# A four-layer decoder trunk on one core: recurrent layer's weights one use ahead, state rows turned later, twelve small tiles for nine

## Chip, cores and metric

The kernel runs on one core of one Trainium2 chip. The metric is the device time of one execution in microseconds; several runs are taken and their median is given. Matmul operands are fp32 bits split into two halves (a rounded upper part and the remainder, both of type fp32r), so that each product of 128 rows takes three matmuls.

## What is computed

The reference is one inference step of four layers with the same skeleton, for 1024 prompt rows and 8 times 4 sample rows (1056 columns here, since the kernel holds activations transposed, features on partitions):

```python
for i in range(DEPTH):            # kinds: conv, attention, recurrent, conv
    mp, ... = mixer_of_kind(yp, ...)
    ms, ... = mixer_of_kind(ys, ...)
    yp = layer_norm(ALPHA * yp + mp, ln_g[i], ln_b[i])
    ys = layer_norm(ALPHA * ys + ms, ln_g[i], ln_b[i])

def rglru_mixer(...):             # the recurrent layer, "C"
    u, z = split(x @ w_in); uc = causal_dwconv(u, buf, conv_w) + conv_b
    r = sigmoid(uc blocks @ w_a + b_a); i = sigmoid(uc blocks @ w_x + b_x)
    a = exp(log_a(r)); b = sqrt(1 - a*a) * (i * uc)
    h = scan(a, b)                # h[t] = a[t]*h[t-1] + b[t]
    return (silu(z) * h) @ w_out, h[-1], last rows of u
```

The short-conv layer ("A") is `(silu(z) * b_gate * conv(c_gate * h)) @ w_out`. Each A and C layer also returns a few state rows (last rows before the convolution, last hidden state).

## The kernel before, in words

Features are cut into 8 chunks of 128 (index c), columns into 3 parts of 352 (index j). One **dense step** is 24 matmuls of 128x352: chunk c of the output for part j, over 8 input chunks, three matmuls each (`dense_steps`). The stages follow each other: layer A (`layer_a`), its out-projection with residual and norm (`out_phase`), layer B (attention), out-projection 1, layer C (`layer_c`, some 232 us), out-projection 2, the second layer A, and `final_phase`, the last out-projection, which turns its result to rows before the norm.

Order. All but the attention's core is recorded, not issued: every call goes through `Rec` (line 310 is where the recorded call is issued, so nearly all work has that line). Each recorded operation has a place in the record and a due time (its place, shifted by the constants in `AHEAD`). `Rec.lay` then walks a small model of the engines: an operation may start when its inputs are done and a buffer of its ring is free; of those able on an engine the one due first is taken. The order found is written out; each engine runs its list strictly in that order. SP issues nearly all transfers, in one list too.

Buffers are rings: `w` (3 tiles, split weights ready for TensorE), `ws` (5 tiles in the later layers, staging for weights, convolution inputs `g`, rows to be stored), `c` (small work tiles), `big` and `x` (18 tiles of a whole chunk); in PSUM `mm` (5 banks, dense steps) and `aux` (3 banks, convolution sums, transposes, statistics).

Weights. `load_w` loads 128 columns of weights into `ws`, ScalarE rounds them into `w` (CAST `w<-ws`), VectorE or GpSimd (by the table `WLO`) writes the remainder (TENSOR_TENSOR `w<-ws,w`). `layer_a` and `out_phase` record these loads two or three uses ahead; `layer_c` records each where it is used:

```python
W = self.get_w(("c", c), lambda: self.load_w(...))   # conv_in, line 1089
WA[n] = weights(n)                                   # gates, line 1135
W = self.load_w(win[:, D + c * P:...], ("z", c))     # gate_out, line 1185
```

`ORDER_C` (line 2211) lists the steps of layer C: `u` for `conv_in` of a chunk, `g` for its gates and scan, `z` for the gated output.

State rows. `put_rows` (line 935) turns the 18 or 36 columns of `SC` to rows by 8 transposes on TensorE into two `aux` banks, copies them to a `ws` tile on VectorE and stores them. `layer_a` and `layer_c` call it as their last step.

The final phase sums squares with `squares` (line 892): ScalarE squares three row pieces with an accumulator; the squared values go to a `c` tile of up to 512 columns and are not read.

Of the kernel before, what the change touches and what calls it, by code (L numbers as in the profile page):

```python
# [9 lines left out]
F32 = mybir.dt.float32  # L10
F32R = mybir.dt.float32r
I32 = mybir.dt.int32
AF = mybir.ActivationFunctionType
# [5 lines left out]
P = 128  # L19
D = 1024  # L20
# [478 lines left out]
class Trunk:  # L499
    def __init__(self, ctx, tc, io):  # L500
        self.ctx, self.tc, self.nc, self.io = ctx, tc, tc.nc, io
        self.rec = Rec(tc)

    @contextmanager
    def part(self):
# [25 lines left out]
        nc.vector.memset(self.ones_m, 1.0 / D)  # L531
        self.ones_r = ones

    def work(self, stack, nws, ncc):

        self.nwork = getattr(self, "nwork", 0) + 1
        self.nws = nws
        self.ws = Ring(self.rec, self.pool(f"ws{self.nwork}", nws, stack), "ws", nws) if nws else None
        self.wx = self.ws
        self.cc = Ring(self.rec, self.pool(f"c{self.nwork}", ncc, stack), "c", ncc)  # L540
# [16 lines left out]
    def wsl(self, w=1088, dt=F32):  # L557
        return self.ws.tile([P, 1088], dt, name="ws")[:, 0:w]

    def ct(self, w=512, dt=F32):  # L560
        return self.cc.tile([P, 512], dt, name="c")[:, 0:w]

    def cst(self, name, dst):
        a, b = COLS[name]
# [41 lines left out]
    def fetch(self, items):  # L606
        for key, fn in items:
            self.pre[key] = fn()
# [76 lines left out]
    def out_phase(self, pm, wsrc, U, X, ln, lp, res=None, done={}, spill=None, final=None, nxt=()):  # L685
# [3 lines left out]
        nc = self.nc  # L689
# [5 lines left out]
        W = {}  # L695
# [69 lines left out]

        running, late = [], {}
        for c, j in order:
            if c not in W:
                take(c)
            sl = slice(j * TC, (j + 1) * TC)  # L770
            xh, xl = X[c][:, 0, sl].bitcast(F32), X[c][:, 1, sl].bitcast(F32)
            k = kt[:, sl]
            if j == 0 and NCH - c <= self.nws - 2 and c >= 4:
                late[c] = self.wsl(T)
            y = done[c, j] if (c, j) in done else late[c][:, sl] if c in late else self.ct(TC)
            x = self.ct(TC)
            if (c, j) not in done:
                ps = self.mm(pm)[:, 0:TC]
                self.dense(ps, W[c], U, j, k if c else None)
                if res is None:  # L780
                    stt(out=ps, in0=xl, scalar=ALPHA, in1=ps, op0=ALU.mult, op1=ALU.add)
                    stt(out=y, in0=xh, scalar=ALPHA, in1=ps, op0=ALU.mult, op1=ALU.add)
                else:
                    nc.sync.dma_start(x, res[c][:, sl], rk=[("x", ln - 1, c, j)])
                    stt(out=y, in0=x, scalar=ALPHA, in1=ps, op0=ALU.mult, op1=ALU.add)
            if j == 2 and c >= 4:
                self.fetch(nxt[c - 4:c - 3])
            if c == 0:
                kp = self.aux(pm)[:, 0:TC]
                nc.tensor.matmul(kp, self.ones_m, y, start=True, stop=True)  # L790
                nc.scalar.activation(k, kp, AF.Copy, scale=-8.0 * NCH)
            d = ss[:, 0, sl] if c == 0 else y
            if c == 0 or (c, j) in done:
                stt(out=d, in0=k.bitcast(F32), scalar=0.125, in1=y, op0=ALU.mult, op1=ALU.add)
            if c == 0:
                nc.scalar.activation(ss[:, 1, sl], d, AF.Square)
            else:
                e0, e1 = (nc.gpsimd if c in s else nc.vector for s in SUMS[ln])
                e0.tensor_add(ss[:, 0, sl], ss[:, 0, sl], d)
                nc.scalar.activation(x, d, AF.Square)  # L800
                e1.tensor_add(ss[:, 1, sl], ss[:, 1, sl], x)
            if c not in late:
                nc.sync.dma_start(self.dd[c][:, sl], d, wk=[("d", ln, c, j)])
            for g in running:
                next(g, None)
            if c == NCH - 1:
                g = norm(j)
                next(g)
                running.append(g)
# [4 lines left out]
    def final_phase(self, pm, wsrc, U, X, ln, lp):  # L814


        nc, io = self.nc, self.io
# [6 lines left out]
        sq = lp.tile([P, 3, 3, 3], F32, name="fsq")  # L824
        W, R, gb = {}, {}, []

# [65 lines left out]
        def squares(j, n, c0, c1):  # L892
            nk = stat[:, j, 0:3]
            if n == 0:
                nc.vector.tensor_reduce(out=nk, in_=sm[:, j, 0:4].rearrange("p c i -> p i c"), axis=AX.X, op=ALU.add)
                nc.vector.tensor_scalar(out=nk, in0=nk, scalar1=-2.0 / D, scalar2=0.0, op0=ALU.mult, op1=ALU.add)
            for i in range(3):
                x = half(j, c0 // 4, i)[:, c0 % 4 * P:(c1 - 1) % 4 * P + P]
                nc.scalar.activation(self.ct((c1 - c0) * P), x, AF.Square, bias=nk[:, i:i + 1], accum_out=sq[:, j, i, n:n + 1])

        running = []
        for c, j in [(c, j) for c in range(4) for j in range(3)] + [(c, j) for j in range(3) for c in range(4, NCH)]:
            if c not in W:
                take(c)
            sl = slice(j * TC, (j + 1) * TC)
# [20 lines left out]
            if c == NCH - 1:  # L926
                g = norm(j)
# [19 lines left out]
    def layer_a(self, pm, a, X, lp, side=None, nxt=()):  # L947
        nc, io = self.nc, self.io
        stt = nc.vector.scalar_tensor_tensor
        win = io["a_w_in"][a]  # L950
# [69 lines left out]
            nc.vector.tensor_copy(SC[:, c, 2:18].rearrange("p (b t) -> p b t", t=2), gs[:, :, 4:6])  # L1020
        for _ in side or ():
            pass
        self.put_rows(pm, SC, 18, [(0, 2, io["o_conv_a_prompt"][a, 0]), (2, 18, io["o_conv_a_sample"][a].rearrange("b t f -> (b t) f"))])
        return U

    def first_a(self, a):
# [51 lines left out]
    def layer_c(self, pm, X, lp):  # L1078
# [7 lines left out]
        def conv_in(c, js):  # L1086

            if c not in UC:
                W = self.get_w(("c", c), lambda: self.load_w(win[:, c * P:(c + 1) * P], ("c", c)))
                g = self.wsl(1083)  # L1090
                nc.vector.memset(g[:, 0:3], 0.0)
                gs = g[:, 1027:1083].rearrange("p (b t) -> p b t", t=7)
                nc.vector.tensor_copy(gs[:, :, 0:3], self.PT[:, c, R_SC:R_SC + 24].rearrange("p (b t) -> p b t", t=3))
                uc = self.view2(self.big(F32R))
                UC[c], GT[c] = uc, (W, g, gs)
# [36 lines left out]
        def gates(c):  # L1132
            n, i = c // 2, c % 2
            if i == 0:
                WA[n] = weights(n)
                H[n] = self.big()[:, 0:2 * T].rearrange("p (a n) -> p a n", a=2)
            wax, h2, ucs = WA[n], H[n], (UC[c - i], UC[c - i + 1])
            rr, ii = [], []
# [43 lines left out]

        def gate_out(c):
            h2, i = H[c // 2], c % 2
            W = self.load_w(win[:, D + c * P:D + (c + 1) * P], ("z", c))
            u = self.view2(self.big(F32R))
            U[c] = u
            for j in range(3):
# [8 lines left out]

            nc.sync.dma_start(win_s[c, 0:508, :], cache[c, 4:512, :], rk=[("z", c)])
        UC, GT, WA, H = {}, {}, {}, {}
        win_s = io["o_nsa_win_sample"][0].rearrange("b t c g d -> b t (c g d)")  # L1200
        cache = io["cache_nsa_win"][0].rearrange("b t c g d -> b t (c g d)")
        for x in ORDER_C.split():
# [2 lines left out]
                conv_in(c, [int(j) for j in x[2:] or "012"])  # L1205
            else:
                (gates if x[0] == "g" else gate_out)(c)
        self.put_rows(pm, SC, 36, [(0, 3, io["o_lru_conv_prompt"][0, 0]), (3, 27, io["o_lru_conv_sample"][0].rearrange("b t f -> (b t) f")),
                                   (27, 28, io["o_lru_h_prompt"][0]), (28, 36, io["o_lru_h_sample"][0])])
        return U  # L1210

    def first_c(self):
# [1118 lines left out]
def trunk(ctx, tc, io, layers="ABCA"):  # L2331
# [37 lines left out]
            left = k.attend(B, bs, io["b_w_out"][0], xd)  # L2369
    with ExitStack() as c1:  # L2370
        lp = k.small(c1)
        k.work(c1, 5, 9)
        pm = banks(c1, "pm_1")
        k.rec.forget()
        k.later = 1
# [47 lines left out]
```

## Time and profile before

| | |
|---|---|
| median of 3 runs | 2428.99 us (2427.99 to 2431.45) |
| profiled execution | 2425.75 us, span of its records 2423.7 us |
| busy in the span | PE 2305.6, DVE 1583.6, ACT 1203.7, POOL 959.3 us |
| mean granted clock of TensorE | 0.977 of full speed |
| layer C, 1600 to 1832 us | PE 225.55, DVE 176.77, ACT 175.85, POOL 97.93 us |

The profile is one execution of the program. PE is TensorE's matmul, PEld its weight load, DVE VectorE, ACT ScalarE, POOL GpSimd, SPq the list of transfers on SyncE. A tile stands by its ring's name. Idle time before an instruction is put down to the work that ended it.

### The profile page before, as it was taken

To read this page: it belongs to the slowest core of one execution; us is meant where nothing else is said; L and a number is where in the kernel's file an instruction comes from. 1 tells how busy PE (TensorE), PEld (TensorE's weight loads), DVE (VectorE), ACT (ScalarE), POOL (GpSimd) and SP (SyncE) were. 2 spreads that over 40 slices of the span, in tenths; PEclk is the share of its full clock that TensorE was granted. 3 is DMA by queue.
4 is the path that set the end of the run, shared out by engine and by line. 5 is a ranking of instruction groups with operands and counts; after the bars stand their busy time and mean duration, and the time that the engine had idled before them with its cause. 6 is when DMAs were issued, how large, how long until landed. Compare 5 with 4: busy or idle time off the path is not lost. (4 is left out here: it accounts for less than half of the span.)

```text
span 2423.7 us, 41400 instructions
## 1 busy us (share of the span) xinstructions
PE 2305.6 (95%) x14801; PEld 2234.8 (92%) x14801; DVE 1583.6 (65%) x3686; ACT 1203.7 (50%) x2757; POOL 959.3 (40%) x1070
## 2 busy tenths in 40 slices
PE   8999997997989989999999999989999999999996
PEld 8999997996888879999999989989999999999996
DVE  5786875575358877777777777787765753433336
ACT  3211111234438878888888883487863442222233
POOL 3454543213137765565555552333463320000131
PEclk9999999997999999999999999999999999999998
DMA  7999988347356752111111234331113321111112
GB/s 260 351 350 338 321 291 281 98 151 245 104 175 230 247 201 56 33 47 43 47 48 41 78 123 124 117 103 53 53 47 118 99 67 53 44 44 53 35 46 72
DMA packets 334642, 320.34 MB, mean 132 GB/s; under 512 B 19462, under 2 KB 301542, under 8 KB 324964
## 3 DMA queue, kind: packets, MB, share of 16 engines
q1 hardware_dynamic: 325220, 250.58, 33.4%
q0 software_dynamic: 9216, 67.11, 7.4%
q8 instruction: 117, 1.92, 0.3%
q14 instruction: 89, 0.73, 0.1%
HBM read 237.31 MB, written 84.48 MB: 133 GB/s over the span
## 5 line engine op out<-in xcount | busy, mean ns | idle before, releaser
L310 PE MATMUL mm<-x,w 128*128 128x352 f32 x5760 | 948.9, 326 | 29.6 <-DVE ws L310 10.3
L310 PEld LDWEIGHTS mm<-x,w 128*128 128x128 f32 x5760 | 936.4, 190 | 36.6 <-DVE w L310 7.6
L310 PE MATMUL mm<-big,w 128*128 128x352 f32 x2208 | 375.4, 325 | 1.0 <-ACT c L310 1.0
L310 PEld LDWEIGHTS mm<-big,w 128*128 128x128 f32 x2208 | 357.2, 189 | 2.8 <-ACT c L310 1.3
L310 POOL TENSOR_TENSOR w<-ws,w 128x1024 fp32r<-128x1024 f32 (+1 forms) x43 | 104.8, 2438 | 445.8 <-ACT w L310 426.7
L1968 DVE TENSOR_TENSOR c<-T,c 128x512 fp32r<-128x512 f32 (+1 forms) x320 | 204.7, 648 | 49.3 <-ACT c L1964 44.9
L1964 ACT CAST c<-T 128x512 fp32r<-128x512 f32 (+1 forms) x320 | 174.3, 551 | 59.3 <-PE T L1960 37.7
L310 ACT CAST w<-ws 128x1024 fp32r<-128x1024 f32 (+2 forms) x116 | 120.3, 1038 | 163.3 <-PE mm L310 119.4
L641 PE MATMUL D<-x,w 128*128 128x352 f32 x1008 | 195.5, 330 | 2.2 <-DVE big L2095 2.2
L1870 PE MATMUL A<-big 128*128 128x320 f32 (+11 forms) x832 | 181.5, 334 | 3.4 <-DVE ast L1895 1.6
L1975 PE MATMUL O<-c,big 128*128 128x256 f32 x1056 | 180.4, 291 | 0.5 <-ACT c L1964 0.2
L310 POOL TENSOR_TENSOR big<-big,ws 128x1024 f32<-128x1024 f32 (+1 forms) x38 | 89.6, 2358 | 199.0 <-DMA big<-in_cache_nsa_kv,idx 103.9
L641 PEld LDWEIGHTS D<-x,w 128*128 128x128 f32 x1008 | 159.8, 188 | 5.7 <-DVE big L2095 3.5
L310 DVE TENSOR_TENSOR big<-big 128x256 f32<-128x256 f32 (+3 forms) x204 | 150.5, 758 | 21.7 <-POOL big L310 20.3
L310 DVE TENSOR_TENSOR w<-ws,w 128x1024 fp32r<-128x1024 f32 (+2 forms) x73 | 93.9, 1286 | 105.6 <-ACT w L310 104.8
L310 ACT CAST big<-aux 128x352 fp32r<-128x352 f32 (+3 forms) x116 | 45.4, 399 | 229.9 <-DVE aux L310 160.6
L1975 PEld LDWEIGHTS O<-c,big 128*128 128x128 f32 x1056 | 147.2, 189 | 2.5 <-DVE c L1968 0.7
L1928 POOL TENSOR_SCALAR pr<-pr,G,ast 128x32 f32<-128x32 f32 (+6 forms) x192 | 125.6, 668 | 47.1 <-DVE ast L1939 41.3
L1870 PEld LDWEIGHTS A<-big 128*128 128x128 f32 x832 | 134.3, 193 | 10.0 <-PE A L1870 2.2
L310 ACT ACTIVATE aux<-ws,PT 128x352 f32<-128x352 f32 (+2 forms) x72 | 42.7, 593 | 172.5 <-DVE ws L310 167.9
L1924 ACT ACTIVATE pr<-pr,ast 128x32 f32<-128x32 f32 (+6 forms) x192 | 118.4, 619 | 18.3 <-DVE ast L1895 17.4
L310 DVE SCALAR_TENSOR_TENSOR c<-c,mm 128x352 f32<-128x352 f32 x125 | 64.1, 515 | 92.3 <-ACT c L310 54.6
(286 smaller groups left out, 4032.7 us busy)
## 6 DMA issues: line engine op xcount, KB each, us to landing
ws<-in_a_w_in SPq DMA_DIRECT2D x64, 512.0 KB
raw<-big SPq DMA_DIRECT2D x128, 256.0 KB
big<-raw SPq DMA_DIRECT2D x128, 256.0 KB
c<-dd SPq DMA_DIRECT2D x48, 176.0 KB
xs<-x SPq DMA_DIRECT2D x24, 352.0 KB
x<-xs SPq DMA_DIRECT2D x8, 1056.0 KB
ws<-in_a_w_out SPq DMA_DIRECT2D x16, 512.0 KB
ws<-in_c_w_in SPq DMA_DIRECT2D x16, 512.0 KB
```

What stands on the lines that cost most here:

```text
L310: getattr(real, name)(*[f(x) for x in a], **{q: f(x) for q, x in k.items()})
L641: self.nc.tensor.matmul(ps, a, b, start=n == 0, stop=n == 23 and last)
L1870: nc.tensor.matmul(o, q[:, hl, i * P:(i + 1) * P], k, start=m == 0, stop=m == 1)
L1924: nc.scalar.activation(S[:, a:a + m], S[:, a:a + m], AF.Exp, bias=st[:, k:k + 1], scale=-1.0, accum_out=st[:, 3 + k:4 + k])
L1928: nc.gpsimd.tensor_scalar(S[:, a:a + m], S[:, a:a + m], G[:, i, 16 * k + h:16 * k + h + 1], st[:, 6 + k:7 + k], op0=ALU.mult, op1=ALU.mult)
L1964: nc.scalar.copy(x["H"][:, 0:n], x["tp"][:, 0:n])
L1968: nc.vector.tensor_sub(x["L"][:, 0:n], x["tp"][:, 0:n], x["H"][:, 0:n].bitcast(F32))
L1975: nc.tensor.matmul(O, v, M[:, y * P:(y + 2) * P], start=done[0] == 0, stop=done[0] == total - 1)
```

## The change

Four parts. (1) In layer C a table `todo` of all weight sets in order of use is made, and `take` records the set asked for and also the next one. (2) `put_rows` is no longer called at the end of a layer but kept as `self.rows` and called in the out-projection that follows, ahead of the step (c, j) = (2, 0). (3) In the layers after the attention a `c` tile has 384 columns instead of 512, and there are 12 instead of 9. (4) The unread squares of the final phase, up to 512 columns wide, go to an `aux` bank.

```diff
@@ out_phase, in the loop over (c, j)
+            if (c, j) == (2, 0) and self.rows:
+                self.rows()
+                self.rows = None
@@ final_phase
-                nc.scalar.activation(self.ct((c1 - c0) * P), x, AF.Square, bias=nk[:, i:i + 1], accum_out=sq[:, j, i, n:n + 1])
+                nc.scalar.activation(self.aux(pm)[:, 0:(c1 - c0) * P], x, AF.Square, bias=nk[:, i:i + 1], accum_out=sq[:, j, i, n:n + 1])
...
+            if (c, j) == (2, 0):
+                self.rows()
@@ layer_a (and layer_c likewise)
-        self.put_rows(pm, SC, 18, [(0, 2, io["o_conv_a_prompt"][a, 0]), (2, 18, io["o_conv_a_sample"][a].rearrange("b t f -> (b t) f"))])
+        self.rows = lambda: self.put_rows(pm, SC, 18, [(0, 2, io["o_conv_a_prompt"][a, 0]),
+                                                       (2, 18, io["o_conv_a_sample"][a].rearrange("b t f -> (b t) f"))])
@@ layer_c
-                W = self.get_w(("c", c), lambda: self.load_w(win[:, c * P:(c + 1) * P], ("c", c)))
+                W = take(("c", c))
...
-                WA[n] = weights(n)
+                WA[n] = take(("g", n))
...
-            W = self.load_w(win[:, D + c * P:D + (c + 1) * P], ("z", c))
+            W = take(("z", c))
...
+        def fetch(key):
+            w, c = key
+            if key not in self.pre:
+                self.pre[key] = weights(c) if w == "g" else self.load_w(win[:, (w == "z") * D + c * P:(w == "z") * D + (c + 1) * P], key)
+
+        def take(key):
+
+            fetch(key)
+            i = todo.index(key)
+            for k in todo[i + 1:i + 2]:
+                fetch(k)
+            return self.pre.pop(key)
@@ trunk
-        k.work(c1, 5, 9)
+        k.work(c1, 5, 12, 384)
```

The new record gives another order. At the end of the first layer A, TensorE's list before (-) and now (+), with `SC` the state columns, `mm<-big` the out-projection's dense steps and `aux<-c,ones_m` its column sums:

```order
 L310 MATMUL aux<-c 128x8
 L310 MATMUL mm<-x,w 128x352 x2226
-L310 MATMUL aux<-idf,SC 18x128 x8
 L310 MATMUL mm<-big,w 128x352 x36
 L310 MATMUL aux<-c,ones_m 128x352
```

The transposes have left the place between the layer's last dense step and the out-projection's first; they stand after its sixth step now. VectorE's list at the same place, where `big<-aux,big` writes the remainder of layer A's last output chunk, and `c<-x,mm` ends the first residual:

```order
 L310 TENSOR_TENSOR big<-aux,big 128x352
 L310 SCALAR_TENSOR_TENSOR c<-mm,c 128x352
-L310 COPY ws<-aux 18x512
 L310 TENSOR_TENSOR aux<-c,aux 128x320
-L310 COPY ws<-aux 18x512
+L310 TENSOR_TENSOR w<-ws,w 128x1024
 L310 TENSOR_TENSOR big<-aux,big 128x320
 L310 TENSOR_TENSOR aux<-c,aux 128x8x4
+L310 SCALAR_TENSOR_TENSOR mm<-x,mm 128x352
 L310 TENSOR_TENSOR big<-aux,big 128x32
-L310 SCALAR_TENSOR_TENSOR mm<-x,mm 128x352
 L310 SCALAR_TENSOR_TENSOR c<-x,mm 128x352
```

Both copies are gone from here, and a weight remainder has come in ahead of the last pieces. TensorE's list where layer C begins, before, with buffer numbers (`w_17980` and `w_17853` are the sets of chunks 1 and 0; `mm_18125` is their part j = 1, `mm_18272` and `mm_18284` are j = 2):

```order
L310 MATMUL mm_18125<-x_17915,w_17853 128x352 x3
L310 MATMUL mm_18125<-x_17936,w_17853 128x352 x3
L310 MATMUL mm_18272<-x_17772,w_17980 128x352 x3
L310 MATMUL mm_18272<-x_17793,w_17980 128x352 x3
L310 MATMUL mm_18284<-x_17772,w_17853 128x352 x3
L310 MATMUL mm_18284<-x_17793,w_17853 128x352 x3
```

and now (`w_18069` is the set of chunk 2, `mm_18266` and `mm_18295` its parts j = 0 and 1, `mm_18306` and `mm_18318` part j = 2 of chunks 1 and 0):

```order
L310 MATMUL mm_18266<-x_17915,w_18069 128x352 x3
L310 MATMUL mm_18266<-x_17928,w_18069 128x352 x3
L310 MATMUL mm_18295<-x_17772,w_18069 128x352 x3
L310 MATMUL mm_18295<-x_17819,w_18069 128x352 x3
L310 MATMUL mm_18306<-x_17772,w_17996 128x352 x3
L310 MATMUL mm_18306<-x_17819,w_17996 128x352 x3
L310 MATMUL mm_18318<-x_17772,w_17866 128x352 x3
L310 MATMUL mm_18318<-x_17819,w_17866 128x352 x3
```

Thirty matmuls of chunk 2 now stand ahead of the first ones on part j = 2, and twelve more between those; before, all of chunk 2 stood behind them. ScalarE's list in layer C around a weight set for a `z` step, before (`c<-mm,sp` empties a gate's dense step, `ws<-mm` a convolution's):

```order
L310 ACTIVATE c_19190<-mm_19170,sp_17077 128x352
L310 COPY ws_18633<-mm_19085 128x8x4
L310 ACTIVATE c_19198<-mm_19180,sp_17077 128x352
L310 ACTIVATE aux_19201<-ws_18633,PT_400 128x376
L310 ACTIVATE c_19205<-c_19144,sp_17077 128x352
L310 CAST w_19208<-ws_18865 128x1024
```

and now, where the same set is `w_19096`:

```order
L310 CAST w_19096<-ws_18856 128x1024
L310 ACTIVATE c_19003<-c_19003,sp_17077 128x352
L310 COPY ws_18872<-mm_19008 128x352
L310 COPY ws_18872<-mm_19054 128x352
L310 ACTIVATE aux_19121<-ws_18872,PT_400 128x352
L310 ACTIVATE aux_19124<-ws_18872,PT_400 128x352
L310 COPY ws_18872<-mm_19089 128x320
L310 COPY ws_18872<-mm_19089 128x8x4
```

The cast stood behind the last gate step that precedes its use; it now stands ahead of the nine steps that precede its use (three of 24 matmuls, six of 6).

## Rows read from the trace of the kernel before

**Rows 1.** The page, part 1: busy time and share of the span.
```profile
PE 2305.6 (95%) x14801; PEld 2234.8 (92%) x14801; DVE 1583.6 (65%) x3686; ACT 1203.7 (50%) x2757; POOL 959.3 (40%) x1070
```
**Rows 2.** Waits of TensorE, 413 to 440 us: sum, times, longest.
```profile
PE aux L310 <- DVE big L310: 14.1, 2, 12.3
```
**Rows 3.** Windows: stretch, length, busy PE, PEld, DVE, ACT, POOL; clock, DMA, GB/s.
```profile
1600.00:1832.00 232.00, 225.55 (x1372) 224.06 (x1373) 176.77 (x336) 175.85 (x296) 97.93 (x85) 0.98 0.19 54
...
1680.00:1700.00 20.00, 20.00 (x112) 20.00 (x112) 16.04 (x31) 13.22 (x21) 8.03 (x8) 0.88 0.19 54
```
**Rows 4.** Timeline of TensorE, end of the first layer A: start, length, [idle before].
```profile
402.05 11.85 PE L310 MATMUL mm<-x,w 128*128 128x352 f32 x72 [2.02 <-DVE ws L310]
426.22 1.02 PE L310 MATMUL aux<-idf,SC 128*18 128x128 f32 x4 [12.33 <-DVE big L310]
...
429.74 7.07 PE L310 MATMUL mm<-big,w 128*128 128x352 f32 x36
436.65 0.76 PE L310 MATMUL aux<-c,ones_m 128*128 128x352 f32 x2
```
**Rows 5.** Timeline of VectorE at the same place.
```profile
425.64 0.53 DVE L310 TENSOR_TENSOR big<-aux,big 128x352 fp32r<-128x352 f32 x1 [2.41 <-ACT big L310]
...
429.36 0.67 DVE L310 COPY ws<-aux 18x512 f32<-18x512 f32 x1
```
**Rows 6.** Timeline of TensorE, out-projection 1 into layer C.
```profile
1586.43 0.43 PE L310 MATMUL mm<-x,w 128*128 128x352 f32 x1 [2.07 <-ACT x L310]
1588.34 9.35 PE L310 MATMUL mm<-x,w 128*128 128x352 f32 x47 [1.48 <-DVE x L310]
1598.87 0.59 PE L310 MATMUL mm<-x,w 128*128 128x352 f32 x2 [1.19 <-ACT w L310]
1600.16 11.52 PE L310 MATMUL mm<-x,w 128*128 128x352 f32 x70 [0.70 <-DVE w L310]
1611.51 5.94 PE L310 MATMUL mm<-big,w 128*128 128x352 f32 x36
```
**Rows 7.** Timeline of VectorE there.
```profile
1578.10 0.16 DVE L310 TENSOR_SCALAR stat<-stat 128x3 f32<-128x3 f32 x1
...
1594.21 1.19 DVE L310 TENSOR_TENSOR x<-ws,x 128x352 fp32r<-128x352 f32 x1
...
1598.89 1.21 DVE L310 TENSOR_TENSOR w<-ws,w 128x1024 fp32r<-128x1024 f32 x1
...
1609.60 1.01 DVE L310 TENSOR_TENSOR big<-aux,big 128x320 fp32r<-128x320 f32 x3
```
**Rows 8.** Timeline of SyncE's transfers there.
```profile
1593.69 0.40 SPq L310 DMA_DIRECT2D ws<-in_c_w_in  x1
```
**Rows 9.** Timeline of TensorE inside layer C.
```profile
1678.02 0.96 PE L310 MATMUL mm<-x,w 128*128 128x352 f32 x2 [2.74 <-ACT w L310]
1679.28 25.55 PE L310 MATMUL mm<-x,w 128*128 128x352 f32 x142 [0.30 <-DVE w L310]
...
1749.61 24.62 PE L310 MATMUL mm<-x,w 128*128 128x352 f32 x142 [2.26 <-DVE w L310]
```
**Rows 10.** ScalarE in layer C, groups by line: busy, mean ns, idle before.
```profile
L310 ACT ACT_TABLE_LOAD x35 | 44.9, 1283 | 1.6 <-DVE c L310 1.1
```
**Rows 11.** Timeline of ScalarE at the first wait of rows 9.
```profile
1676.93 1.03 ACT L310 CAST w<-ws 128x1024 fp32r<-128x1024 f32 x1
```
**Rows 12.** Timeline of TensorE and VectorE in the last 26 us.
```profile
2398.45 4.00 PE L310 MATMUL mm<-big 128*128 128x352 f32 x24
...
2404.13 0.51 DVE L310 SCALAR_TENSOR_TENSOR c<-c,mm 128x352 f32<-128x352 f32 x1
...
2407.89 0.56 DVE L310 TENSOR_REDUCE fsum<-aux 128x3 f32<-128x384 f32 x1 [1.06 <-PE aux L310]
```
**Rows 13.** Timeline of ScalarE there: one square and the read of its accumulator.
```profile
2388.55 0.62 ACT L310 ACTIVATE c<-big,fstat 128x384 f32<-128x384 f32 x1
2389.08 0.19 ACT L310 ACTIVATION_READ_ACCUMULATOR c<-big,fstat 128x1 f32 x1
```

More of the change, by code (lines that the diff above doesn't have):

```diff
@@ L501, in __init__ @@
         self.ctx, self.tc, self.nc, self.io = ctx, tc, tc.nc, io
-        self.rec = Rec(tc)
+        self.rec, self.rows = Rec(tc), None
     @contextmanager
@@ L532, in setup, with work @@
         self.ones_r = ones
-    def work(self, stack, nws, ncc):
+    def work(self, stack, nws, ncc, cw=512):
         self.nwork = getattr(self, "nwork", 0) + 1
-        self.nws = nws
+        self.nws, self.cw = nws, cw
         self.ws = Ring(self.rec, self.pool(f"ws{self.nwork}", nws, stack), "ws", nws) if nws else None
@@ L558, in wsl, with ct @@
         return self.ws.tile([P, 1088], dt, name="ws")[:, 0:w]
-    def ct(self, w=512, dt=F32):
-        return self.cc.tile([P, 512], dt, name="c")[:, 0:w]
+    def ct(self, w, dt=F32):
+        return self.cc.tile([P, self.cw], dt, name="c")[:, 0:w]
     def cst(self, name, dst):
@@ L1199, in layer_c @@
         UC, GT, WA, H = {}, {}, {}, {}
+        todo = []
+        for x in ORDER_C.split():
+            c = int(x[1])
+            key = ({"u": "c"}.get(x[0], x[0]), c // 2 if x[0] == "g" else c)
+            if key not in todo:
+                todo.append(key)
+        def fetch(key):
[8 more added lines that the diff above has]
+            return self.pre.pop(key)
         win_s = io["o_nsa_win_sample"][0].rearrange("b t c g d -> b t (c g d)")
@@ L1207, in layer_c @@
                 (gates if x[0] == "g" else gate_out)(c)
-        self.put_rows(pm, SC, 36, [(0, 3, io["o_lru_conv_prompt"][0, 0]), (3, 27, io["o_lru_conv_sample"][0].rearrange("b t f -> (b t) f")),
-                                   (27, 28, io["o_lru_h_prompt"][0]), (28, 36, io["o_lru_h_sample"][0])])
+        self.rows = lambda: self.put_rows(pm, SC, 36, [(0, 3, io["o_lru_conv_prompt"][0, 0]), (3, 27, io["o_lru_conv_sample"][0].rearrange("b t f -> (b t) f")),
+                                                       (27, 28, io["o_lru_h_prompt"][0]), (28, 36, io["o_lru_h_sample"][0])])
         return U
```

## The prediction

> **What bounds the kernel now.** I read the page's busy table first: TensorE is busy 2305.6 us of the span of 2423.7 [rows 1], so 118 us are idle, and every other engine has a third or more of the span free. A change can therefore pay in two ways only: by filling TensorE's idle stretches, or by keeping its clock up. Next I read its waits and timeline stage by stage, at the four places that the edits touch. In [rows 2] the reader sees that the start of the first out-projection loses 14.1 us to VectorE; [rows 3] show that layer C itself leaves only 232 - 225.55 = 6.45 us of TensorE idle, with VectorE and ScalarE each near 176 us, and that for 20 us in it the granted clock was 0.88 although TensorE was busy all 20.00. The price of work is taken at the best rate: 36 matmuls in 5.94 us [rows 6], 0.165 us each.
>
> The profiled execution took 2425.75 us, 2.0 more than its span. The median of the runs is 2428.99, so 3.24 above it; terms are worked out on the profile and taken off the median.
>
> **A, state rows out of the first out-projection's start: -3 us.** Now TensorE ends the layer at 402.05 + 11.85 = 413.90, its next instruction is a transpose, and that gets its bank only at 426.22, after VectorE's remainder at 425.64 [rows 4, 5]. The dense steps behind it need the same remainder for their last chunk, but only in 3 of each 24 matmuls. With the transposes gone, 21 matmuls run at once (about 3.5 us, to 417.4), and then TensorE waits for the same 425.64 + 0.53 = 426.17. So the wait is shortened by 3.5 us and not removed. Is that worth 3.5 at the end? The next thing that must come is the first column sum, at 436.65 [rows 4], which needs the first residual. VectorE, from 429.36 on [rows 5], loses two copies and gets one weight remainder (1.21 for that size, [rows 7]); six pieces of at most 0.53 and this remainder stand up to the residual's end: 429.36 + 3.2 + 1.2 = 433.8 at the latest. The column sum comes 2.9 us earlier, 3.7 if the pieces are as short as some of them, and the eight transposes still have to be run, twice 1.02 [rows 4], of which I count about half, since the first four ran here in time that is a wait otherwise. I take -3; the ends are -6 (the wait's 3.5 and all that the clock loses in the 7.07 for 36 matmuls) and 0. At the other two ends of layers no such wait stands, and the move is costed at nothing: eight transposes are covered by nothing, but they are run in either place.
>
> **B, out-projection 1 into layer C: -6 us.** TensorE waits here 2.07 + 1.48 for the last part of `x`, then 1.19 + 0.70 for the weights of chunk 2 [rows 6]: 5.44 us. Behind the second wait 47 matmuls take 9.35 us instead of 47 x 0.165 = 7.76, another 1.6 for the clock. Ceiling 7.0. These matmuls of chunk 2 need only parts of `x` that are long done; what is late is their weights, whose load was issued at 1593.69 [rows 8] and whose remainder was written at 1598.89 [rows 7]. Recorded one use ahead, the set is there earlier, and 42 of its matmuls (6.9 us) now stand ahead of or among the first ones on part j = 2; that covers 2.07 and 1.48. The cost: on VectorE the remainder, 1.21 us, stands ahead of the norm's chain of part 2 (small operations such as that at 1578.10, then the `x` piece at 1594.21, [rows 7]) and delays that. 7.0 - 1.2 = 5.8, taken as 6; the low end is -7. The gates' matmuls wait for `big` at 1609.60 + 1.01 [rows 7] against their start of 1611.51 [rows 6], so some of this can be held up there; if all is, 0.
>
> **C, inside layer C: -6 us.** Three waits stand here, 2.74 for the cast of a `z` set, 0.30 for its remainder and 2.26 for a remainder of the next set [rows 9]: 5.3 us. The first reads as follows: the cast starts at 1676.93, takes 1.03 [rows 11], and TensorE starts at 1678.02. ScalarE reached it late, since it stood behind all evictions of the gates. Now it stands nine steps ahead of its use, so the wait goes. After the waits 142 matmuls take 25.55 and 24.62 us [rows 9] where 142 x 0.165 = 23.4: 2.1 + 1.2 lost to the clock. Ceiling 8.6. I take the waits and a fifth of the clock's part, since I can't tell from these rows what else lowers it. The twelve tiles of 384 columns cost no instruction (no piece in these layers but the squares is wider); with them four loads of ScalarE's tables drop out of the program's list, 4 x 1.28 = 5.1 us of ScalarE by [rows 10], which is hidden behind TensorE and counts only as slack: in layer C ScalarE is busy 176 of 232. What is late next are evictions by ScalarE and VectorE. Ends: -9, and 0 if those take over.
>
> **D, the tail: -1.5 us.** VectorE's residual of chunk 6 stood at 2404.13, behind six wide norm operations, though its matmuls had ended when the last step began at 2398.45 [rows 12]. In the new order it stands before them. Behind the wide operations (which end 0.5 later, at about 2404.6) there are then a sum of 0.56 and the last residual, 0.51, then three transposes, 0.77 at the rate of [rows 4]: the last sum starts at about 2406.4 instead of 2407.89 [rows 12]. Nothing but the norm of the last part follows. Ends -2 and 0.
>
> **E, squares into `aux` banks: nothing.** They are written and never read. A square has a bank for 0.53 us up to the read of its accumulator and 0.19 for that [rows 13], and 27 of them come in nine groups of three, which is the whole ring of three banks. TensorE needs a bank for each transpose; five banks of `mm` let dense matmuls go on meanwhile, which is the cover.
>
> Sum: -3 - 6 - 6 - 1.5 = -16.5, so 2428.99 - 16.5 = **2412.5 us**. With the terms' own bounds its range is 2406 to 2419.
>
> **Rivals.**
> *The next engine ends the waits.* With VectorE and ScalarE busy three quarters of layer C [rows 3], the waits for weights become waits for evictions: C gives nothing, B half. -3 - 3 - 1.5 = -7.5: 2421.5. For it: no eviction is removed. Against: 56 us of slack on each in layer C. Chance 0.20.
>
> *Squares hold the banks.* Each of nine groups makes a transpose wait for one square, 0.72 [rows 13]: +6.5, so 2419.0. Against it: the tail's squares come while TensorE has little to do. Chance 0.07. The Trainium skill ("Perfetto Trace Analysis", section Matmuls) says that independent groups of matmuls should rotate through different PSUM banks, so that the emptying of one overlaps the next; by it a ring lent to ScalarE is this rival.
>
> *Casts at the head of the list, slower.* There are three `w` tiles. A cast recorded one use early stands in ScalarE's list ahead of evictions; if its tile is still in use it stops them, and TensorE with them when the `mm` banks are full. Layer C has 20 weight sets (8, 4 and 8). At one cast's length each, 1.03 [rows 11], that is +20.6; with C's gain lost, 20.6 - 10.5 = +10: 2439. It decides from 10.5 / 20 = 0.53 us for each set. Against it: two sets are held at a time, and the third tile is free when the set before the current one is used up. Chance 0.05.
>
> *Chunk 2's remainder comes late.* VectorE now meets it before 1578.10. Were its load no earlier than before, VectorE would stand until 1598.89, 20.8 us, of which the 42 matmuls give back 6.9; with A, C and D that is +13.9 - 10.5: 2432.4. It needs an issue as late as 1593.69 [rows 8]; but the load is now listed ahead of the spills it stood behind. Chance 0.04.
>
> *It doesn't do what it says.* The ring of three keeps the casts where they were, B and C are nothing: 2424.5, no change within what can be told. Chance 0.06. The Trainium skill ("Perfetto Trace Analysis", Optimization Strategy) reads a gap that repeats as too few buffers. By that, order alone would not help here; the trace so far only bears out that the wait for `w` recurs [rows 9].
>
> **How the numbers follow.** My forecast has 0.58. Its own range, the rivals at 2419.0, 2421.5 and 2424.5, and A to D at their full -24 set 2405 to 2426; outside are the two late-weight rivals and spill-over of each case. A measurement of this kernel can tell about 0.2%, 4.9 us: faster means under 2424.1. Forecast and the first two rivals, less a part of their upper spread, give 0.80 faster; the last rival, that of chunk 2 and this spread 0.12 the same; casts and other new waits 0.08 slower.
>
> **What would show it.** A: in the first out-projection TensorE starts dense matmuls near 413.9, still waits until about 426, and has its first column sum near 433. B: no wait for `w` between 1586 and 1600, less than 2 us for `x`. C: TensorE's idle time in layer C falls from 6.45 us to about 1, and the 142 matmuls behind a `z` set take less than 25 us. D: the last sum starts about 7.9 us after the last 24 matmuls began, not 9.4. I am wrong if TensorE's new waits in layer C are for `mm` or `c` and add up to as much, if ScalarE shows idle time that ends with a `w` tile coming free, or if transposes in the final phase wait for ScalarE.

## The result, and the profile after

The median is 2405.08 us (2404.01 to 2407.38, 4 runs) against 2428.61 for the kernel before in the same comparison: 23.5 us less, ratio 0.9902 (95% interval 0.9885 to 0.9919). A later comparison gave 0.9917 (0.9896 to 0.9937); every ratio here is to the kernel before in the same comparison. The forecast was faster by 16.5, and the gain is 7 us larger. The time lies below the forecast's own range, 2406 to 2419, and on the low edge of the wider one, 2405 to 2426: 0.9902 x 2428.61 = 2404.8, a hair under 2405.

Part 1 of the page of the changed kernel, which answers to [rows 1]:

```profile
PE 2303.5 (96%) x14801; PEld 2233.7 (93%) x14801; DVE 1573.5 (65%) x3686; ACT 1197.4 (50%) x2753; POOL 963.3 (40%) x1070
```

TensorE is busy 2.1 us less; the span of this profile is 2405.1, so its idle time fell from 118 to 101.6 us. To see where, I number TensorE's dense matmuls of 352 columns (9504 in every kernel) and note when each starts. A stretch runs between two of them; the table gives how much longer (+) or shorter (-) each kernel's profile is there than the profile before. Stretches are named by the clock of the kernel before.

| kernel | 0-412 | 412-520 | 520-1500 | 1500-1612 | 1612-1820 | 1820-1900 | 1900-1960 | 1960-2402 | tail |
|---|---|---|---|---|---|---|---|---|---|
| changed kernel | +4.5 | -1.7 | -1.5 | -7.3 | -8.8 | +2.1 | -4.1 | +0.2 | -2.1 |
| after_again (the same) | +3.9 | +0.7 | -3.0 | -5.8 | -8.8 | +1.4 | -4.0 | +0.2 | -2.2 |
| e1_weights | +4.9 | +2.5 | -4.7 | -5.9 | -8.3 | +7.9 | +0.4 | 0.0 | -0.2 |
| e2_rows | +7.4 | +1.1 | +0.7 | +0.5 | -2.4 | +0.4 | +2.5 | -0.1 | -0.2 |
| e3_tiles | +4.9 | +4.2 | -3.7 | +1.6 | 0.0 | +0.9 | -4.1 | +0.3 | -1.9 |
| e4_squares | +3.4 | +1.4 | -4.5 | +0.5 | -2.3 | 0.0 | +0.4 | +0.3 | -1.9 |
| e5_norows | +1.7 | +2.2 | +0.1 | -7.3 | -8.8 | +7.0 | +5.3 | +0.3 | -1.9 |
| e6_noweights | +3.6 | +2.0 | +0.1 | -0.1 | -0.3 | +1.4 | -4.0 | +0.2 | -2.2 |
| e7_notiles | +2.1 | -2.6 | +0.3 | -6.0 | -8.6 | +0.4 | +2.5 | -0.1 | +0.3 |
| e9_c_rows | +10.1 | +2.1 | -3.8 | -5.8 | -8.4 | +1.4 | -4.0 | +0.3 | -2.2 |
| e10_a_rows | +4.3 | +0.6 | +0.3 | -7.3 | -8.8 | +6.5 | +4.7 | +0.2 | -2.2 |
| e11_rows_big | +8.3 | -1.9 | -3.6 | -5.8 | -8.8 | +0.5 | -3.8 | +0.3 | -2.2 |
| e12_out_first | +4.1 | +0.2 | -4.7 | -7.2 | -8.0 | +0.5 | -3.9 | +0.3 | -2.2 |
| e13_out_ahead | +10.3 | +0.7 | -6.3 | -5.8 | -8.6 | +0.8 | +5.4 | +0.2 | -1.9 |
| e18_one_set | +2.9 | -0.8 | +0.9 | -7.2 | -8.3 | +0.8 | +6.5 | +0.2 | -2.2 |
| e19_stage_big | +1.8 | -2.7 | -0.8 | -7.2 | -8.7 | +0.8 | -3.1 | +0.2 | -2.2 |

Read the first column first. Up to 412 us no part of the change has touched the program, yet all sixteen profiles are 1.7 to 10.3 us later there than the one the prediction was worked out on. That stretch moves by itself, and the profile before was the earliest of the seventeen. So two profiles' spans must not be subtracted (that gives 18.6), only the stretches where the change acts.

**Layer C** (1612 to 1820). Its window in the kernel before and in the changed one: length, busy time of TensorE, its weight loads, VectorE, ScalarE, GpSimd; granted clock, DMA share, GB/s. Before:

```profile
1612.16:1820.01 207.85, 201.56 (x1224) 200.13 (x1223) 154.16 (x285) 163.00 (x273) 90.45 (x79) 0.98 0.17 49
```

Changed:

```profile
1606.24:1805.34 199.10, 196.70 (x1220) 195.54 (x1219) 166.69 (x311) 161.74 (x280) 90.53 (x81) 1.00 0.18 51
```

8.75 us less: 3.9 are idle time of TensorE (6.29 to 2.40), 4.9 are the same dense matmuls done in less busy time, with the granted clock at 1.00, not 0.98. That second number depends on the profile it is taken from. Five kernels keep the waits for weights here, and their busy time moves from profile to profile: 201.56 before, 201.00 in e3, 200.33 in e6, 198.84 in e4 and, the lowest, in e2:

```profile
1621.84:1827.25 205.41, 198.32 (x1220) 196.99 (x1219) 153.14 (x284) 162.80 (x273) 90.46 (x79) 0.99 0.15 44
```

Their mean is 200.0, so the clock's part is 3.3 us on average, 1.6 to 4.9 in the single profiles; by the table's column the whole gain is 7.6 on average (-8.6 in the twelve profiles with the weights ahead, -1.0 in these five). The waits of the changed kernel there (sum, times, longest) name no weights any more; what is left waits for evictions:

```profile
PE mm L310 <- DVE c L310: 1.1, 1, 1.1
PE mm L310 <- ACT c L310: 1.1, 2, 0.7
PE mm L310 <- DVE big L310: 0.2, 1, 0.2
```

TensorE's timeline shows it where [rows 6, 9] had breaks (start, length, matmuls, idle before). From out-projection 1 into layer C, and behind the `z` set that had waited 2.74:

```profile
1581.21 2.02 PE L310 MATMUL mm<-x,w 128*128 128x352 f32 x11 [0.83 <-DVE x L310]
1584.33 21.42 PE L310 MATMUL mm<-x,w 128*128 128x352 f32 x132
...
1670.34 23.30 PE L310 MATMUL mm<-x,w 128*128 128x352 f32 x144
```

**The first out-projection**, TensorE as in [rows 4], and two operations of VectorE:

```profile
404.70 13.74 PE L310 MATMUL mm<-x,w 128*128 128x352 f32 x81
418.28 3.53 PE L310 MATMUL mm<-big,w 128*128 128x352 f32 x21
431.36 5.03 PE L310 MATMUL mm<-big,w 128*128 128x352 f32 x15 [9.56 <-ACT big L310]
438.48 0.86 PE L310 MATMUL aux<-c,ones_m 128*128 128x352 f32 x2 [2.08 <-DVE c L310]
```

```profile
425.59 1.22 DVE L310 TENSOR_TENSOR big<-big,ws 128x1024 f32<-128x1024 f32 x1 [6.31 <-DMA big<-in_cache_nsa_kv,idx]
...
431.34 0.53 DVE L310 TENSOR_TENSOR big<-aux,big 128x352 fp32r<-128x352 f32 x1 [0.56 <-ACT big L310]
```

It runs as forecast, 21 matmuls, a wait, 15, the first sum: 438.48 - 431.34 = 7.1 us behind the remainder, where [rows 4, 5] had 11.0. But the remainder itself is 5.7 us later than at 425.64. Of that, 4.5 is the shift of the first 412 us; the rest goes with VectorE's wait for a gather's DMA, work of another layer in its list, which was shorter before:

```profile
419.45 1.52 DVE L310 TENSOR_TENSOR big<-big,ws 128x1024 f32<-128x1024 f32 x1 [4.82 <-DMA big<-in_cache_nsa_kv,idx]
```

**The end of out-projection 2**, SyncE's list, with `c<-xc` and `c<-dd` the columns stored earlier that residual and norm need. Before:

```profile
1914.02 0.53 SPq L310 DMA_DIRECT2D c<-xc  x1
1914.60 0.90 SPq L310 DMA_DIRECT2D c<-dd  x2
1915.55 0.43 SPq L310 DMA_DIRECT2D c<-xc  x1
...
1926.93 0.32 SPq L310 DMA_DIRECT2D c<-dd  x1
1927.34 0.38 SPq L310 DMA_DIRECT2D c<-xc  x1
```

Changed:

```profile
1900.81 1.53 SPq L310 DMA_DIRECT2D c<-xc  x3
1902.38 2.55 SPq L310 DMA_DIRECT2D c<-dd  x5
...
1906.15 0.38 SPq L310 DMA_DIRECT2D c<-xc  x1
1908.23 3.51 SPq L310 DMA_DIRECT2D ws<-in_a_w_in  x2
```

With twelve tiles these loads go out together: 5.3 us from first to last, not 13.3. Two waits of TensorE that stood behind them in the kernel before are gone:

```profile
1933.85 0.90 PE L310 MATMUL mm<-x,w 128*128 128x352 f32 x4 [1.58 <-DVE w L310]
1935.56 1.62 PE L310 MATMUL aux<-ones_m,big 128*128 128x1 f32 x12 [0.81 <-DVE big L310]
```

**The tail**, TensorE's last 24 matmuls (the first twelve of them) and VectorE, as in [rows 12]:

```profile
2381.73 2.09 PE L310 MATMUL mm<-big 128*128 128x352 f32 x12
```

```profile
2382.00 0.52 DVE L310 SCALAR_TENSOR_TENSOR c<-c,mm 128x352 f32<-128x352 f32 x1 [0.16 <-PE mm L310]
...
2388.13 0.51 DVE L310 SCALAR_TENSOR_TENSOR c<-c,mm 128x352 f32<-128x352 f32 x1
2389.72 0.56 DVE L310 TENSOR_REDUCE fsum<-aux 128x3 f32<-128x384 f32 x1 [1.08 <-ACT ws L310]
```

Chunk 6's residual stands ahead of the wide operations; the last sum is 8.0 us behind the start of the last 24 matmuls (2381.73), before 9.4.

### The profile page after: what moved, and what is told of

Same layout as the page of the kernel before. It is cut to its first block, busy times and chain, and to the rows that moved or that the text cites. A ratio compares the mean times of both kernels' runs of the same rounds, so it can differ in the third digit from the quotient of the medians.

```text
span 2405.1 us, 41388 instructions
## 1 busy us (share of the span) xinstructions
PE 2303.5 (96%) x14801; PEld 2233.7 (93%) x14801; DVE 1573.5 (65%) x3686; ACT 1197.4 (50%) x2753; POOL 963.3 (40%) x1070
## 5 line engine op out<-in xcount | busy, mean ns | idle before, releaser
L310 DVE TENSOR_TENSOR big<-big 128x256 f32<-128x256 f32 (+3 forms) x204 | 140.8, 711 | 24.1 <-POOL big L310 22.5
```

The lines of the kernel that those rows point to most:

```text
L310: getattr(real, name)(*[f(x) for x in a], **{q: f(x) for q, x in k.items()})
```

## The experiments

Three kernels have one part of the change, one all but the rows.

**e1_weights**: `take` and `todo` in `layer_c` alone.

> The weights one use ahead alone; rows, tiles and squares as before. Measured in the changed kernel: TensorE's progress through its dense matmuls gains 7.3 us between out-projection 1 and the start of layer C, 8.8 inside layer C, 3.6 from out-projection 2 into the last layer, and about 2 in the tail. Theory 1: the first two are this part's alone, so this kernel is 14 to 17 us faster than before. Rival (tiles): with nine small tiles the earlier sets run into evictions that wait for a tile; only the 7.3 stays, 6 to 9 us faster. Rival (plan): any change of the record gives another order, and the gains are the luck of one order; then anything between 0 and 15, with the gain in places that have no weights of layer C.

Ratio 0.9977 (0.9964 to 0.9990), 5.6 us. Both gains of layer C are there (-5.9, -8.3), and 7.9 are given back at once where out-projection 2 starts. No theory had that.

**e2_rows**: `self.rows` alone.

> The moved state rows alone. The changed kernel gained 2.6 us at the start of the first out-projection, paid 0.9 for the transposes, and gained 4.1 where layer B begins and 3.6 at the end of out-projection 2. Theory 1: only the first two are the rows', 1 to 3 us faster. Rival: the rows also free VectorE and the transfers behind them, so the 4.1 and the 3.6 are theirs too: 8 to 10 us faster.

0.9986 (0.9974 to 0.9998), 3.4 us: theory 1, a little above. Nothing is gained at the end of out-projection 2.

**e3_tiles**: `k.work(c1, 5, 12, 384)` and the squares in `aux`.

> Twelve tiles of 384 and the squares in aux banks, nothing else. Theory 1: only the tail's 1.5 to 2 us, since no wait of layer C was for a tile. Rival (tiles): evictions run further ahead, layer C's waits for weights shrink because ScalarE and VectorE reach the casts earlier, and 5 us or more of the 8.8 in layer C appear here.

0.9976 (0.9962 to 0.9990), 5.8 us. Layer C is unchanged (0.0), so the rival falls; but 4.1 appear at the end of out-projection 2, which theory 1 didn't have.

**e5_norows**: all but `self.rows`.

> All of the change except the moved state rows. Theory 1: as the changed kernel less the 1 to 3 us of the first out-projection, about 20 to 22 us faster than before. Rival of the rows: 13 to 16 us faster, with the 4.1 at the start of layer B and the 3.6 at the end of out-projection 2 gone. The first 412 us have the same lists as before, so the profile also tells how far that stretch moves by itself (it differed by 4.6 us between the two kernels so far).

0.9971 (0.9960 to 0.9982), 7.0 us, less than either expected. Without moved rows the start of out-projection 2 costs 7.0 and its end 5.3. The parts don't add up, and the knot lies in out-projection 2. The next four ask which rows matter, and what the other parts are worth when the rest is there.

**e10_a_rows**: the change, but at the end of `layer_c`

```diff
-        self.rows = lambda: self.put_rows(pm, SC, 36,
+        self.put_rows(pm, SC, 36,
```

> The change, but layer C turns its state rows at its own end again; both layers A still leave theirs to the out-projection. Theory 2 (formed on the runs so far): with the weights ahead, TensorE reaches the end of layer C before the last hidden states and before ScalarE has rounded the weights of out-projection 2; in the kernels that turn the rows there, that start cost 7.3 and 8.2 us against the kernel before, in the changed kernel 1.4. So moving these 8 transposes is worth about 6 us only together with the weights: this kernel is 6 us or more slower than the changed kernel, 14 to 18 us faster than before, and the loss lies in its profile at the first steps of out-projection 2. Where the transfer list then also stands for a weight tile at the end of out-projection 2, as in the kernel without moved rows (a wait of 5.4), up to 9 more. Theory 1 (rows matter at the first out-projection alone): like the changed kernel, 22 to 24 us faster than before.

0.9976 (0.9964 to 0.9989), 5.8 us: theory 2, with the further loss of up to 9 that it names. By the table layer C's rows alone decide 14 us, 5 at the start and 9 at the end. The start, TensorE:

```profile
1809.52 0.60 PE L310 MATMUL aux<-idf,SC 128*36 128x128 f32 x4
1811.67 0.59 PE L310 MATMUL mm<-big,w 128*128 128x352 f32 x2 [1.56 <-ACT w L310]
1814.34 5.34 PE L310 MATMUL mm<-big,w 128*128 128x352 f32 x22 [2.08 <-POOL w L310]
```

The out-projection waits for its weights. SyncE's list in the same kernel, at the start and at the end of that phase:

```profile
1809.11 9.07 SPq L310 DMA_DIRECT2D ws<-in_c_w_out  x3
...
1909.50 8.01 SPq L310 DMA_DIRECT2D ws<-in_a_w_in  x2
1917.56 1.05 SPq L310 DMA_DIRECT2D c<-xc  x2
```

Weight loads stand at its head for 9.07 and 8.01 us, and the columns for the norm stand behind. SyncE's waits between 1805 and 1820 us say for what: for GpSimd's remainders, which read the `ws` tiles that the next loads want.

```profile
SPq L310 <- POOL w L310: 7.7, 2, 4.7
```

**e9_c_rows**: the reverse, at the end of `layer_a` (and no call in `final_phase`):

```diff
-        self.rows = lambda: self.put_rows(pm, SC, 18,
+        self.put_rows(pm, SC, 18,
```

> The reverse: only layer C leaves its rows to the out-projection, both layers A turn them at their end. Theory 2: keeps everything but what the first out-projection gains: between the layer's last step and the 30th matmul of the out-projection the kernels with rows in place took 2 to 4 us more than before ran there and those with moved rows 1 to 3 us less, and 0.9 for the transposes comes back, so this kernel is 3 to 4 us slower than the changed one, 18 to 21 us faster than before. Theory 1: the rows' whole effect is here, 15 to 17 us faster than before as far as the kernel without moved rows (7 us faster) tells.

0.9923 (0.9904 to 0.9942), 18.7 us: theory 2.

**e7_notiles**: the change with `k.work(c1, 5, 9)` and squares in `c` tiles.

> Weights ahead and rows moved, but nine tiles of 512 and the squares in them. Theory 2: the tiles bring only the 3.6 us at the end of out-projection 2 (the kernel with the tiles alone shows them too) and 1.5 to 2 in the tail: 4 to 6 us slower than the changed kernel, 17 to 20 us faster than before. Rival (tiles carry layer C): the 8.8 us in layer C shrink; 10 to 14 us faster than before.

0.9949 (0.9930 to 0.9969), 12.4 us. The number is the rival's, but not its reason: layer C keeps its 8.6, so the rival's mechanism falls. The end of out-projection 2 loses 6.6 against the changed kernel, not 3.6.

**e6_noweights**: the change with the `layer_c` of before.

> Rows moved and small tiles, each weight set of layer C where it was. Theory 2: nothing is gained between out-projection 1 and the end of layer C; what is left is 3 to 4 at the first out-projection, 3.6 at the end of out-projection 2 and 1.5 to 2 in the tail: 7 to 10 us faster than before. Rival (parts only work together): all of it gone, 0 to 5 us faster.

0.9982 (0.9971 to 0.9993), 4.4 us, in the rival's range. But the parts do work by themselves (-4.0 at the end of out-projection 2, -2.2 in the tail, nothing in layer C); this profile shows +2.0 at the first out-projection, where 3 to 4 had been expected off.

**e11_rows_big**: e10, and one line of `put_rows`:

```diff
-        rows = self.wsl(D)
+        rows = self.big(w=D) if n == 36 else self.wsl(D)
```

> As the kernel in which layer C turns its state rows at its own end (5.5 us faster than before), with one edit: those rows are gathered in a tile of the ring big instead of ws. Transposes, copies and stores stay. Theory 3: what cost 5 us at the start of out-projection 2 and 9 at its end is the ws tile: in the record the rows take one of the five ahead of the weights of the out-projection, and loads stand at the head of SyncE's list until one comes free (9.1 and 8.0 us in that kernel's trace). Then this edit brings most of it back: 15 to 20 us faster than before, the start of out-projection 2 within 2 us of the changed kernel. Rival (place): the transposes and copies themselves, between the last scans and the first dense steps, cost it: 4 to 8 us faster than before, as without the edit. In between, about 10 to 12, if the start comes back and the end does not.

0.9907 (0.9887 to 0.9926), 22.6 us. All of it is back, more than theory 3 gave, at the start (+0.5) and the end (-3.8), with transposes still at the end of layer C. It was the staging tile.

**e12_out_first**: e10, and ahead of `put_rows`:

```diff
+        self.fetch(self.first_out(2, io["c_w_out"][0]))
```

> As the kernel in which layer C turns its state rows at its own end, with one edit: the first two weight sets of out-projection 2 are recorded ahead of the rows. The rows still take a ws tile. Theory 3 (the tile, by its place in the record): the sets get their tiles first, so the start of out-projection 2 comes back, 5 us or more, and the whole is 10 to 18 us faster than before. Rival (place of the transposes): 4 to 8 us faster than before.

0.9911 (0.9893 to 0.9929), 21.6 us, above theory 3's 10 to 18. The rows keep their `ws` tile, but are recorded behind the two sets; that is enough, at both ends.

**after_again**: the changed kernel, in the same comparison.

> The changed kernel once more, for the three others of this call and for how far its stretches move by themselves. From the stretches of the runs so far: -2.9 at the first out-projection, -6 to -7.3 into layer C, -8.6 in it, +0.6 to 1.4 at the start of out-projection 2, -3.6 at its end, -2.1 in the tail; together 22 to 24 us faster than before. Its first 412 us should again differ by several us from those of its first profile, though the lists are the same.

0.9917 (0.9896 to 0.9937), 20.2 us, a little under the 22 to 24 expected. So layer C's rows needn't have been moved: e11 and e12 are as fast.

**e13_out_ahead**: the changed kernel, with these sets one use ahead too.

```diff
+            if i == len(todo) - 1:
+                self.fetch(self.first_out(2, io["c_w_out"][0]))
             return self.pre.pop(key)
```

> The changed kernel, and at the last set of layer C also the first two sets of out-projection 2 recorded one use ahead. What is left to gain is the 1.04 us wait and the 0.6 to 1.4 us at that start: 0 to 2 us faster than the changed kernel by all theories. If casts at the head of ScalarE's list stop evictions (the rival of the prediction), 2 to 5 us slower than the changed kernel, with waits of TensorE for ScalarE's c tiles in the last 20 us of layer C.

0.9955 (0.9937 to 0.9972): 9 us less than the change gains, against every expectation. Not where the casts are: the start of out-projection 2 is 0.6 to 1.3 better. The loss is at the end, where TensorE, SyncE and VectorE show:

```profile
1928.44 0.56 PE L310 MATMUL aux<-ones_m,big 128*128 128x1 f32 x2 [5.83 <-DVE big L310]
```

```profile
1904.87 8.64 SPq L310 DMA_DIRECT2D ws<-in_a_w_in  x2
1913.57 1.04 SPq L310 DMA_DIRECT2D c<-xc  x2
```

```profile
1917.86 0.52 DVE L310 SCALAR_TENSOR_TENSOR c<-c,mm 128x352 f32<-128x352 f32 x1 [8.72 <-DMA c<-xc]
```

It is e10's order again: a second weight load ahead of the columns. SyncE's waits between 1900 and 1920 us end with the landing of a load and with a GpSimd remainder that has read its tile:

```profile
SPq L310 <- DMA ws<-in_a_w_in: 4.6, 2, 4.2
SPq L310 <- POOL w L310: 3.6, 1, 3.6
```

**e18_one_set**: e13, and in `first_a`, whose sets are recorded inside out-projection 2:

```diff
-for w in (0, 2, 3)]
+for w in ((0,) if self.later else (0, 2, 3))]
```

> As the changed kernel with the out-projection's first sets also one use ahead (9 us faster than before, and 11 slower than the changed kernel, all of which lies at the end of out-projection 2, where TensorE waited 5.8 us), with one edit: only one of the three weight sets of the last layer's start is recorded inside out-projection 2, so no second weight load stands in SyncE's list ahead of the spilled columns (c<-xc, c<-dd) that the norm needs. Theory (head of the list): the load of 8.6 us in that list is gone from there, and with it the wait of 5.8; the end of out-projection 2 gains 9 us against that kernel, and the whole is 20 to 25 us faster than before. Rival (the sets themselves, or VectorE's work there, make the wait): it stays, 8 to 12 us faster than before. If the two sets come too late instead, a wait for w of 1 to 4 us at the last layer's first steps, 16 to 20.

0.9950 (0.9933 to 0.9966), 12.2 us: no better, and by its number the rival's. VectorE's wait for the columns is gone and a longer one has come:

```profile
1911.97 4.00 PE L310 MATMUL mm<-x,w 128*128 128x352 f32 x24
...
1926.44 2.85 PE L310 MATMUL aux<-c,ones_m 128*128 128x128 f32 x12 [9.24 <-DVE c L310]
```

With one set there are 24 matmuls to run while VectorE works out the norm, not 48. The edit took the cover with the cause, so it settled nothing.

**e4_squares**: the squares in `aux`, nothing else.

> The squares of the final phase into aux banks, and nothing else: nine tiles of 512 stay. In its order VectorE's residual of chunk 6 already stands ahead of the wide norm operations. If the squares' banks alone free the tail, the stretch behind the last dense matmul is 2.0 us shorter (19.5 instead of 21.5) and the end of out-projection 2 is as before: 1.5 to 2 us faster than before in all, hardly to be told in the median. If the number of tiles does it, the tail stays at 21.5 us. If the squares hold the banks of the transposes (the rival of the prediction), the final phase ahead of it grows by up to 6.5 us.

0.9990 (0.9976 to 1.0004), not to be told from no change, but the profile answers: tail -1.9, end of out-projection 2 +0.4, final phase +0.3. The tail's gain is the squares', the other gain the number of tiles.

**e19_stage_big**: e13, with only the second of the two loads staged in a `big` tile.

```diff
+STAGE = (("a", 1, 2, 0),)
-        st = self.wsl(1024).rearrange("p (k f) -> p k f", k=8)
+        st = (self.big(w=1024) if key in STAGE else self.wsl(1024)).rearrange("p (k f) -> p k f", k=8)
```

> As the kernel with the out-projection's first sets one use ahead too (11 us slower than the changed kernel), with one edit: the second of the two weight loads that stand together in SyncE's list ahead of the spilled columns goes to a tile of the ring big, not ws. All three sets are still recorded inside out-projection 2, so the 48 matmuls that cover the norm stay. In its order the load now stands behind the spilled columns. Theory (a load that waits for a ws tile at the head of SyncE's list): VectorE's wait of 8.7 for the columns and TensorE's of 5.8 go, the end of out-projection 2 gains 9 us, and the whole is 20 to 25 us faster than before, as the changed kernel or up to 1 us better. Rival (other work of that order makes the wait): 8 to 12 us faster than before, the wait of 5 us or more still there.

0.9921 (0.9903 to 0.9939), 19.2 us, just under the theory's 20 and far from the rival's 8 to 12, beside the changed kernel's 20.2 and 23.5. In SyncE's list the columns now go ahead of the load:

```profile
1897.73 0.80 SPq L310 DMA_DIRECT2D c<-xc  x2
1898.62 1.80 SPq L310 DMA_DIRECT2D c<-dd  x4
...
1903.56 0.38 SPq L310 DMA_DIRECT2D big<-in_a_w_in  x1
```

The end of out-projection 2 went from +5.4 to -3.1, 8.5 us, with the sets and the cover kept. That shows the cause. It doesn't beat the changed kernel by anything that can be told.

## Why the prediction had the direction right and the size 7 us short

The prediction's own bounds first. A's low end of -6 is more than its two parts give: 3.5 and, for the clock, 7.07 - 5.94 = 1.1 make 4.6. And 2406 to 2419 isn't what the terms' bounds make, which together run from 2405 to 2429. That 2405 came so close to the time is in part that slip.

**A, the first out-projection: -3 forecast.** Eleven profiles with layer A's rows moved average -0.4 between 412 and 520, six with the rows in place (the one before with 0 among them) +2.1: -2.5, transposes included. The ranges overlap (-2.7 to +2.0 and 0 to +4.2), so the size is an average and no more. The mechanism is in the timeline.

**B, into layer C: -6.** Measured -5.8 to -7.3 in every kernel with the weights ahead, +1.6 to -0.1 without. What parts 5.8 from 7.3 is the granted clock, as the same program shows, the changed kernel's two profiles with the same waits of 2.9 us (columns as for layer C):

```profile
1501.38:1606.24 104.86, 101.92 (x652) 100.58 (x650) 88.48 (x201) 51.52 (x101) 35.50 (x29) 1.00 0.41 132
1501.69:1607.98 106.29, 103.36 (x651) 102.19 (x650) 88.14 (x201) 51.44 (x101) 35.13 (x29) 0.98 0.40 130
```

No wait for `w` is left at the place of [rows 6], and 0.72 + 0.83 for `x`, as forecast. That chunk 2's remainder would come late didn't happen.

**C, inside layer C: -6, measured -8.0 to -8.8** against the one profile before, 7.6 against the mean of the five that keep the waits. This term is mis-sized by 1.6 to 2.8. The waits for weights went as forecast, and 1.4 us of new waits for evictions came. The step that failed is "I take the waits and a fifth of the clock's part": a fifth was 0.7, and that part measured 4.9 against the profile before and 3.3 on average, as much as all that I had found in the two pieces of 142 matmuls. A wait's price here was its idle time and also what the clock took from the work behind it. Why the second part differs between profiles with nearly the same waits (before 4.9, e4 2.1) stays open.

**D, the tail: -1.5, measured -2.1 to -2.2**, by the squares. Its mechanism, residual ahead of the wide operations, is in the rows above. **E:** no transposes waited for squares: the final phase is +0.2 to +0.3 with them in `aux`, and the profile lists no wait of TensorE between 2120 and 2383 us. So that rival falls. The Trainium skill's advice to rotate matmul groups through banks ("Perfetto Trace Analysis", Matmuls) wasn't put to a test, since the three banks were never short.

**The end of out-projection 2: not in the sum, -4.** The step that failed is that the twelve tiles were put at nothing: the prediction saw only the ScalarE time they save, which "counts only as slack". They count where transfers fill `c` tiles: the norm's columns are loaded together, which gains 4 us, in e3 with neither weights nor rows moved (e4 has the squares alone, +0.4). I had looked at instructions and not at which transfers wait for that ring.

**The start of out-projection 2: +1.4 to 2.1**, also missing, as "the move is costed at nothing". Taken alone that is nearly true (e2: +0.4). But with the weights ahead and layer C's rows in place a wait for the out-projection's weights stands here, +6.5 to +7.9 in e1, e5 and e10; the rows' tile, out of the way, let the out-projection's own weights come in time.

Summed as measured: -2.5 - 6.5 - 8.8 + 1.7 - 4.0 - 2.2 = -22.3, between the 23.5 and 20.2 of the two comparisons; with 7.6 for C it is -21.1. Of the rivals, none came. New waits for evictions took 1.4 us in layer C, not the gain. Casts at the head of ScalarE's list do stand there for a `w` tile that TensorE still uses, which the prediction had named as a sign of being wrong, but hardly longer than before. In layer C, before and changed:

```profile
ACT w L310 <- PE mm L310: 5.4, 3, 3.0
ACT w L310 <- PE mm L310: 5.9, 4, 2.0
```

TensorE's waits for ScalarE's `c` tiles are 1.0 and 1.1 us there, so it cost nothing that can be seen. Three `w` tiles were enough: order alone removed TensorE's waits for weights. For the rows and the weight sets a tile elsewhere brought the time back (e11, e19), and for the rows so did order alone (e12). The Trainium skill says that a repeated gap can mean too few buffers ("Perfetto Trace Analysis", Optimization Strategy); on `w` this trace shows another reason, and on `ws` that one beside order.

## What to carry to other kernels

Ask of every tile that a moved step holds which transfer stands behind it in an ordered list; here loads that stood 8 to 9 us at the head of SyncE's list, until a staging tile was free, cost up to 9 us at a place that the edit didn't name. Parts tested alone gave 5.6, 3.4 and 5.8 us and together 20.2 to 23.5, so test a part by taking it out of the whole as well as by putting it in. Before two profiles are subtracted, cut them into stretches and see which move with the same program.

## What was not expected of the hardware

The first 412 us ended 1.7 to 10.3 us later in sixteen profiles than in the one before, with the same instruction lists there; the share of the DMA engines was 0.94 in that window before and after. In layer C the same dense work took 201.56 us of busy time at a granted clock of 0.98 and 196.70 at 1.00, a difference larger than the 3.9 us of idle time that was removed. It isn't a fixed price: the four other kernels that keep waits for weights there took 198.32 to 201.00.
